# A fixed instruction order from the output projection to the first FFN products

## The chip, the cores and the metric

The kernel runs on one core of one Trainium2 chip. Five engines work beside each other, each taking its own instructions in order: TensorE (PE in the profile, PEld for its weight loads), VectorE (DVE), ScalarE (ACT), GpSimd (POOL) and SyncE (SP, which here issues DMAs). The metric is the device time of one execution in microseconds (us), a median over several; less is better.

## The reference

One layer of a transformer-like block on a sequence of 1024 tokens with 1024 channels, all in float32. What matters here is the passage from the mixer's end to the FFN's entry:

```
x = x + g1 * (merged @ w_out)                       # output projection, gated residual
h = rmsnorm(x, ln2_g) * (1.0 + sc2) + sh2           # modulated norm
f = (silu(h @ w_ffn_gate) * (h @ w_ffn_up)) @ w_ffn_down
x = x + g2 * f
```

`w_out` is 1024 x 1024, `w_ffn_gate` and `w_ffn_up` are 1024 x 2816. Before this stand the mixer's input projection, attention and a gated convolution, which the change does not touch.

## The kernel before

Activations are held transposed: 128 channels on the partitions, tokens along the free axis, in two halves of 512 tokens (n = 0, 1). Channel tiles are counted by m or k from 0 to 7.

Every float32 matrix product is made of three passes with operands rounded to the tensor engine's fp32r format: each operand is split into a high part (ScalarE copies it into an fp32r tile, `whi` for a weight) and a low part (VectorE subtracts the high part from the source, `wlo`), and hi x hi, hi x lo and lo x hi are added in one PSUM bank. A product of the output projection is `mm_ch`: 8 channel tiles x 3 matmuls of 128 x 512. PSUM has eight banks, all handed out under the name `e` by `bank()`.

The output projection is made tile by tile (`wo_tile(m, n)`): all eight m for token half 0, then all eight for half 1, with the split weights `wo` kept for the second half. After each product VectorE forms the new residual `x1` (tiles `xb`, line 1055), ScalarE squares it (line 1062), POOL adds the squares into `acc` (line 134, the line of the helper `tt`), and `x1` is written to DRAM. With m = 7 the squares are summed over the channels by small matmuls with a column of ones (lines 1068, 1069), turned into 1/rms by VectorE and by a power on POOL (lines 120, 121, `rs_m`, `rs_r`), and spread over the partitions by matmuls with the identity (line 1073). `norm2` (line 1078) multiplies `x1` by it, and `split_b` (lines 1082, 1083) adds the shift and splits.

The FFN's two input matrices are multiplied by a Strassen-Winograd scheme: tokens, channels and hidden columns are halved, and seven half products (`half_prod`: 4 channel tiles x 3 matmuls, lines 129 to 131) give the four blocks of a pair of hidden column tiles (j, j + 11). Each half product takes one of seven activation factors, in tiles `rh[q]`, `rl[q]` (high and low parts; some of them in tiles named `big`), and one of seven weight factors. Activation factors 0 and 1 are the two channel halves of token half 0; 2 is a block of token half 1; 3 to 6 are sums of blocks, formed in place in `xb` by VectorE and POOL (lines 1139 to 1157). Weight factors s1 to s4 are sums of blocks that POOL forms in tiles `ws` (line 134). `strassen(j, e, src)` does one column pair for the gate (e = 0) or up (e = 1) matrix; before the factors of token half 1 exist, three pairs of products (`PRE`: (0,0), (0,1), (1,0)) with factors 0 and 1 are made ahead. Memory is reused stage by stage: the tiles `ws` lie where `xb` was.

The order of instructions on each engine is found by a planner that simulates the program as it is traced and takes the earliest traced instruction that it holds to be ready. `in_order(i0)` is a helper that already serves the kernel's first stage: it ties every instruction traced since `i0` to the one before it on the same engine, so that these keep the order in which they are written. The three lines that carry the small sums in the code before:

```python
        ss = bank()
        ...
        r = rstd_of(ss[:, :4], 1.0 / D, dp, 4, eng=nc.vector)
        rb = bank()
```

They stand at the end of `wo_tile` and so directly behind the product of m = 7.

Of the kernel before, what the change touches and what calls it, by code (L numbers as in the profile page):

```python
# [28 lines left out]
def block_kernel(tc, x, x_t, cols, ada_1, ada_2, ada_row, w_q, w_kv, w_v1, w_cg, w_a, w_b, w_o, w_g, w_u, w_d, out):  # L29
# [85 lines left out]
    def rstd_of(ss, scale, pool, w, r=None, eng=nc.gpsimd):  # L115

        m = pool.tile([P, 8], F32, tag="rs_m", bufs=3, name=nm("rs_m"))
        if r is None:
# [2 lines left out]
        nc.gpsimd.tensor_tensor(out=r, in0=m[:, :w], in1=nhalf[:, :w], op=ALU.pow)
        return r
# [723 lines left out]
    def mm_ch(ps, w, ah, al, k0=0, k1=KT):  # L846

        for k in range(k0, k1):
            wh, wl = (v[:, (k % 4) * P:(k % 4 + 1) * P] for v in w[k // 4])
# [1 line left out]
            nc.tensor.matmul(ps, wh, rh_, start=(k == 0), stop=False)  # L851
            nc.tensor.matmul(ps, wh, rl_, start=False, stop=False)  # L852
            nc.tensor.matmul(ps, wl, rh_, start=False, stop=(k == KT - 1))  # L853
# [172 lines left out]
    def split(src):  # L1026

        hi = wp.tile([P, 512], F32R, tag="whi", bufs=9, name=nm("whi"))
        lo = wp.tile([P, 512], F32R, tag="wlo", bufs=9, name=nm("wlo"))
        nc.scalar.activation(hi, src, AF.Copy)  # L1030
        nc.vector.tensor_tensor(out=lo, in0=src, in1=hi.bitcast(F32), op=ALU.subtract)  # L1031
# [2 lines left out]
    def tail_raw(m):
        raw = wp.tile([P, 1024], F32, tag="raw", bufs=3, name=nm("raw"))
        nc.sync.dma_start(raw, w_o[m])
        return raw
# [9 lines left out]
    def wo_tile(m, n):  # L1047

        xi = dp.tile([P, 512], F32, tag="xr", bufs=2, name=nm("xr"))
        ns = slice(n * 512, n * 512 + 512)  # L1050
# [11 lines left out]
        nc.scalar.activation(sq, x1, AF.Square)  # L1062
# [4 lines left out]
        for i in range(4):
            nc.tensor.matmul(ss[:, i:i + 1], acc[n][:, i * P:(i + 1) * P], onec, start=True, stop=False)
            nc.tensor.matmul(ss[:, i:i + 1], sq[:, i * P:(i + 1) * P], onec, start=False, stop=True)
        r = rstd_of(ss[:, :4], 1.0 / D, dp, 4, eng=nc.vector)  # L1070
        rb = bank()
        for i in range(4):
            nc.tensor.matmul(rb[:, i * P:(i + 1) * P], r[:, i:i + 1].broadcast_to([P, P]), ident, start=True, stop=True)
        return rb
# [8 lines left out]
        nc.vector.scalar_tensor_tensor(out=lo, in0=x1, scalar=mod[:, 2, m:m + 1], in1=hi.bitcast(F32), op0=ALU.add,  # L1083
                                       op1=ALU.subtract)

    for m in range(KT):
        if m:
            if m < 7:
                raw = tail_raw(m)
                wo += [split(raw[:, c * 512:(c + 1) * 512]) for c in range(2)] if m < 5 else []  # L1090
                if m >= 5:
                    split_wo(raw, dp, 6)
            else:
                split_wo(tail_raw(m), dp, 6)
        rb = wo_tile(m, 0)
# [3 lines left out]
    NJ = NH // 2  # L1099

    def prod(ps, w, q):
        half_prod(ps, w, rh[q], rl[q])

    def load_pair(j, src):
        return load_raw(src[j]), load_raw(src[j + NJ])
# [10 lines left out]
    for g, (j, e) in enumerate(PRE):
        raw = load_raw((w_g, w_u)[e][j])
        p1, p2 = bank(), bank()
        prod(p1, split(raw[:, :512]), 0)
        prod(p2, split(raw[:, 512:]), 1)  # L1120
        if g < 2:
            c11, c21 = ctile(f"c0{e}", cpa), ctile(f"c1{e}", cpa)
            nc.scalar.activation(c21, p1, AF.Copy)
            tt(nc.vector, c11, p2, c21, ALU.add)
            pre[j, e] = (c11, c21)
        else:
            pre[j, e] = (p1, p2)
# [14 lines left out]
    for j in range(4):
        split_b(rh[2][:, j], rl[2][:, j], 4 + j, norm2(4 + j, 1, rb1))
    stt = nc.vector.scalar_tensor_tensor
    xs = lambda e, n, j: xb[e][n][:, j]
    for j in range(4):
        b01 = norm2(j, 1, rb1)
        stt(out=xs(1, 1, j), in0=xs(1, 1, j), scalar=dsh2[:, j:j + 1], in1=b01, op0=ALU.add, op1=ALU.subtract)
        tt(nc.gpsimd, b01, b01, xs(0, 0, j), ALU.subtract)
        stt(out=xs(0, 0, j), in0=xs(0, 0, j), scalar=mod[:, 2, j:j + 1], in1=xs(1, 1, j), op0=ALU.add, op1=ALU.add)  # L1150
        split_f(5, j, xs(0, 0, j))
# [13 lines left out]
    def strassen(j, e, src):  # L1165

        raw = load_raw(src[j])
        a11, a12 = raw[:, :512], raw[:, 512:]
# [19 lines left out]
        c12, c22 = ct(f"c2{e}", 1), ct(f"c3{e}", 1)  # L1188
        p6 = bank()
        prod(p6, split(s2), 5)  # L1190
        tt(nc.vector, c21, p6, c21, ALU.add)
        p5 = bank()
        prod(p5, split(s1), 4)
        tt(nc.vector, c12, p5, c21, ALU.add)
        p7 = bank()
        prod(p7, split(s3), 6)
        tt(nc.vector, c22, p7, c12, ALU.add)
        tt(nc.vector, c21, p7, c21, ALU.add)
        p3 = bank()
        prod(p3, split(s4), 2)  # L1200
        tt(nc.vector, c12, p3, c12, ALU.add)
        p4 = bank()
        prod(p4, split(a22), 3)
        tt(nc.vector, c21, p4, c21, ALU.add)
# [225 lines left out]
```

## Time and profile before

| | |
|---|---|
| time, median of 3 runs | 1906.98 us (1903.57 to 1910.53) |
| profiled execution: time, span | 1906.22 us, 1904.4 us |
| mean granted TensorE clock | 0.984 |
| TensorE busy | 1821.6 us, 96% of the span |
| VectorE, ScalarE, POOL busy | 1333.8, 776.9, 412.6 us |

The span runs from the first instruction's start to the last one's end. The stretch that the change touches lies between about 1138 us (first product of the output projection) and 1320 us (second column pair of the FFN). A row of a timeline gives start, duration, engine, line, operation and what it writes and reads; behind it, in brackets, how long the engine had stood idle and what ended that. A matmul's shown duration overlaps the next one's, so the step from start to start is its real cost. A row of windows gives the stretch, its length, busy time and count for each of PE, PEld, DVE, ACT and POOL, the granted clock, the share of DMA time and GB/s.

### The profile page before, as it was taken

Reading aid. Unit: us, or ns where it says so; the run is one execution under the profiler, and the core shown is the slowest. Engines: PE = TensorE matmul, PEld = TensorE weight load, DVE = VectorE, ACT = ScalarE, POOL = GpSimd, SP = SyncE. Lnnn points to the kernel's source line nnn. Section 1 sums busy time; section 2 is a strip of 40 time slices with the busy share of each in tenths; the row PEclk is TensorE's granted clock in tenths of the full one; section 3 lists DMA queues with packets and bytes.
Section 4 is the critical chain, followed back from the end, with each engine's and each line's share of the span. In section 5 each row is a group of like instructions: output and inputs, shape, how many; then the busy total and the mean of one; then the engine's idle time right before and its main releaser. Section 6 shows DMA issues by size and latency. Waiting matters only on the chain.

```text
span 1904.4 us, 24641 instructions
## 1 busy us (share of the span) xinstructions
PE 1821.6 (96%) x8781; PEld 1510.2 (79%) x8781; DVE 1333.8 (70%) x1895; ACT 776.9 (41%) x1458; POOL 412.6 (22%) x291
## 2 busy tenths in 40 slices
PE   7999999999999999989999999959999999999999
PEld 5787778887788988777888887748888888878787
DVE  6863867779845888877887543479888778743953
ACT  4342643333434655554655322234344434422221
POOL 1043338232320000000000001145544454300000
PEclk9999999999999999999999999979999999999999
DMA  9598542239549556667453545304344334389676
GB/s 388 205 305 285 170 162 83 77 112 326 188 139 241 145 167 176 179 221 238 128 155 106 195 138 166 111 33 149 142 168 162 143 135 169 128 334 322 240 232 221
DMA packets 153968, 351.42 MB, mean 185 GB/s; under 512 B 15195, under 2 KB 54381, under 8 KB 151670
## 3 DMA queue, kind: packets, MB, share of 16 engines
q1 hardware_dynamic: 93888, 234.82, 38.6%
q10 hardware_dynamic: 58950, 111.36, 16.2%
q0 software_dynamic: 1008, 3.67, 0.5%
q8 instruction: 70, 1.15, 0.3%
q14 instruction: 52, 0.43, 0.1%
HBM read 240.21 MB, written 109.58 MB: 184 GB/s over the span
## 4 chain that ended last, share of the span: by engine, by line
PE 78%; DVE 9%; DMA 6%; issue 3%; ACT 1%; POOL 1%; SPq 0%; ACTq 0%; DVEq 0%; POOLq 0%
PE e L129 7%; PE e L130 7%; PE e L131 7%; PE pj L129 5%; PE pj L130 5%; PE pj L131 5%; PE pj L292 5%; PE pj L851 4%; PE pj L852 4%; PE pj L853 4%; PE e L1273 3%; PE e L1271 3%; PE e L1272 3%; PE tr L784 3%; PE o L800 2%
## 5 line engine op out<-in xcount | busy, mean ns | idle before, releaser
L769 DVE TENSOR_TENSOR_SCAN pt<-pt,mk 128x128 f32<-128x128 f32 (+7 forms) x128 | 172.2, 1351 | 55.1 <-ACT pt L765 54.5
L134 POOL TENSOR_TENSOR acc<-acc,sq 128x512 f32<-128x512 f32 x12 | 15.5, 1291 | 660.6 <-ACT sq L1062 660.6
L129 PE MATMUL e<-big,whi 128*128 128x512 f32 x352 | 138.7, 394 | 18.9 <-ACT whi L1030 18.9
L765 ACT ACTIVATE pt<-z,rq 128x512 f32<-128x512 f32 (+1 forms) x192 | 107.9, 579 | 103.8 <-PE z L764 48.7
L134 DVE TENSOR_TENSOR c<-e,c 128x512 f32<-128x512 f32 x154 | 103.2, 683 | 56.2 <-PE e L131 56.0
L130 PE MATMUL e<-big,whi 128*128 128x512 f32 x352 | 138.4, 393 | 0.0
L131 PE MATMUL e<-big,wlo 128*128 128x512 f32 x352 | 138.1, 392 | 0.0
L129 PE MATMUL pj<-big,whi 128*128 128x512 f32 x320 | 125.1, 391 | 4.4 <-ACT whi L468 2.6
L130 PE MATMUL pj<-big,whi 128*128 128x512 f32 x320 | 124.7, 390 | 0.0
L131 PE MATMUL pj<-big,wlo 128*128 128x512 f32 x320 | 124.3, 390 | 0.0
L1271 PE MATMUL e<-f,whi 128*128 128x512 f32 (+1 forms) x319 | 122.6, 385 | 1.7 <-ACT whi L1030 1.3
L1272 PE MATMUL e<-f,whi 128*128 128x512 f32 (+1 forms) x319 | 122.6, 384 | 0.0
L134 POOL TENSOR_TENSOR ws<-raw,raw 128x512 f32<-128x512 f32 x42 | 61.1, 1456 | 279.3 <-DMA raw<-w_cg 132.2
L1273 PE MATMUL e<-f,wlo 128*128 128x512 f32 (+1 forms) x319 | 116.9, 385 | 3.4 <-DVE wlo L1031 3.4
L134 DVE TENSOR_TENSOR wlo<-raw,whi 128x512 fp32r<-128x512 f32 x124 | 92.9, 756 | 37.3 <-ACT whi L468 29.8
L134 DVE TENSOR_TENSOR c<-pj,c 128x512 f32<-128x512 f32 x140 | 92.9, 682 | 32.8 <-PE pj L131 32.6
L292 PE MATMUL pj<-whi,big 128*128 128x512 f32 x352 | 110.6, 400 | 2.9 <-ACT big L275 2.9
L468 ACT ACTIVATE whi<-raw 128x512 fp32r<-128x512 f32 x116 | 72.4, 628 | 93.3 <-PE pj L130 47.7
L788 DVE TENSOR_TENSOR atl<-tr,ath 128x512 fp32r<-128x512 f32 (+1 forms) x192 | 99.6, 548 | 12.5 <-ACT ath L787 10.9
L787 ACT ACTIVATE ath<-tr 128x512 fp32r<-128x512 f32 (+1 forms) x192 | 87.0, 489 | 49.2 <-PE o L799 30.1
L784 PE MATMUL tr<-dm,pt 128*128 128x128 f32 x576 | 96.3, 276 | 10.3 <-DVE atl L788 10.1
L851 PE MATMUL pj<-big,whi 128*128 128x512 f32 x256 | 105.5, 412 | 0.0
(241 smaller groups left out, 5008.1 us busy)
## 6 DMA issues: line engine op xcount, KB each, us to landing
f<-d_f SPq DMA_DIRECT2D x77, 512.0 KB, 4.3
d_f<-fs ACTq DMA_DIRECT2D x70, 512.0 KB, 2.6
raw<-w_cg SPq DMA_DIRECT2D x40, 512.0 KB, 3.6
raw<-w_g SPq DMA_DIRECT2D x24, 512.0 KB, 3.3
raw<-w_u SPq DMA_DIRECT2D x23, 512.0 KB, 3.3
ad<-ada ACTq DMA_DIRECT2D x19, 512.0 KB, 4.9
ada<-ada SPq DMA_DIRECT2D x8, 1024.0 KB, 10.3
d_t<-ts SPq DMA_DIRECT2D x16, 512.0 KB, 5.3
```

Source lines behind the costliest of these rows:

```text
L129: nc.tensor.matmul(ps, wh[:, k, :], fh[:, k, :], start=(k == 0), stop=False)
L130: nc.tensor.matmul(ps, wh[:, k, :], fl[:, k, :], start=False, stop=False)
L131: nc.tensor.matmul(ps, wl[:, k, :], fh[:, k, :], start=False, stop=(k == 3))
L134: eng.tensor_tensor(out=out, in0=a, in1=b, op=op)
L292: nc.tensor.matmul(ps, a, b, start=(k == 0 and q == 0), stop=(k == KT - 1 and q == 2))
L765: nc.scalar.activation(pt[:, off + s0:off + s0 + m], z[:, :m], AF.Sigmoid, scale=rq[:, 1, i, h:h + 1])
L769: nc.vector.tensor_tensor_scan(out=pt[:, rev], data0=pt[:, rev], data1=mk[:, rev], initial=1.0, op0=ALU.mult, op1=ALU.max)
L784: nc.tensor.transpose(tr[:, j * P:(j + 1) * P], pt[:, off + (b0 + j) * P:off + (b0 + j + 1) * P], ident)
L851: nc.tensor.matmul(ps, wh, rh_, start=(k == 0), stop=False)
L1271: nc.tensor.matmul(o, wh, f[:, 0, c], start=(j == 0), stop=False)
L1272: nc.tensor.matmul(o, wh, f[:, 1, c], start=False, stop=False)
L1273: nc.tensor.matmul(o, wl, f[:, 0, c], start=False, stop=(j == NJ - 1))
```

## The change

The whole passage, from the first output projection product to the last half product of the first column pair, is written out in the order in which each engine is to take it, and tied by `in_order`.

- Token half 0: weight tile m + 3 is loaded and weight tile m + 2 split ahead of product m. The residual's input `xr` is loaded from SyncE's queue instead of ScalarE's, one product ahead.
- Small sums: `sum2` stands behind the product after the last one of its token half, and `spread2` one product behind that. For half 0 the last square is added into `acc` by POOL, so that `sum2` has one partner instead of two.
- Token half 1: the FFN weights of four pairs (`PRE` gains (1,1)) are loaded, and split from product 2 to 5; the normalisation and split of half 0 run from product 2 on; the weight sums s1 to s4 of the first column pair are formed in the raw tiles themselves (and one tile `s2`) instead of in `ws`.
- Factors: in place of one factor after another over all four channel tiles, the work goes by column tile j, in small functions (`n_b22`, `n_b12`, `l_b22`, `f_t3`, `f_t2`, `f_lo`), between the half products. The combination for factor 3 is done by POOL with a shift that ScalarE has added earlier.
- The order of half products of pair (0,0) is p3, p6, p5, p7, p4 and no longer p6, p5, p7, p3, p4, behind eight products made ahead instead of six. Its five combinations follow in `strassen`.

```diff
+    def split_next():
+        hi, lo, src = pend_split.pop(0)
+        nc.scalar.activation(hi, src, AF.Copy)
+        tt(nc.vector, lo, src, hi.bitcast(F32), ALU.subtract)
+    def plan_split(src, pool=None, bufs=9):
...
+        pend_split.append((hi, lo, src))
+        return hi, lo
...
-        nc.scalar.dma_start(xi, x_t[m, :, ns])
+        nc.sync.dma_start(xi, x_t[m, :, n * 512:n * 512 + 512])
...
+    def sum2(n, parts):
+        ss = bank()
...
+    def spread2(r):
+        rb = bank()
...
+    xis = {(0, 0): load_xi(0, 0)}
+    wo_weights(1)
+    wo_weights(2)
+    split_next()
+    split_next()
     for m in range(KT):
...
+        nxt = (m + 1, 0) if m + 1 < KT else (0, 1)
+        xis[nxt] = load_xi(*nxt)
+        if m + 3 < KT:
+            wo_weights(m + 3)
+        for _ in range(2 if m + 2 < KT else 0):
+            split_next()
+        ps = wo_prod(m, 0)
+        wo_end(m, 0, ps, xis.pop((m, 0)))
...
+    PRE = [(0, 0), (0, 1), (1, 0), (1, 1)]
...
+    todo = {2: (0,), 3: (1, 2), 4: (3,), 5: (4, 5), 6: (6,), 7: (7,)}
     for m in range(KT):
-        rb1 = wo_tile(m, 1)
-        split_b(bh[:, m], bl[:, m], m, norm2(m, 0, rb))
+        if m + 1 < KT:
+            xis[m + 1, 1] = load_xi(m + 1, 1)
+        if m < 3:
+            pre_weights(m)
+        elif m == 3:
+            pre_weights(3)
+        elif m == 4:
+            ra = load_raw(w_g[0])
+        elif m == 5:
+            rc = load_raw(w_g[NJ])
+        for k in todo.get(m, ()):
+            split_b(bh[:, k], bl[:, k], k, norm2(k, 0, rb))
+            if k >= 4:
+                nc.scalar.activation(xs(1, 0, k - 4), xs(1, 0, k - 4), AF.Identity, bias=mod[:, 2, k:k + 1])
+        if 2 <= m < 6:
+            split_next()
+            split_next()
+        if m == 6:
+            a11, a12, a21, a22 = ra[:, :512], ra[:, 512:], rc[:, :512], rc[:, 512:]
+            s1, s2, s3, s4 = a21, wp.tile([P, 512], F32, name="s2"), a11, a12
+            tt(nc.gpsimd, s3, a11, a21, ALU.subtract)
+            tt(nc.gpsimd, s2, a22, s3, ALU.subtract)
+        ps = wo_prod(m, 1)
+        if m == 0:
+            r = sum2(0, (acc[0],))
+        elif m == 1:
+            rb = spread2(r)
+        sq = wo_end(m, 1, ps, xis.pop((m, 1)))
+    tt(nc.gpsimd, s4, a12, s2, ALU.subtract)
+    tt(nc.gpsimd, s1, a21, a22, ALU.add)
...
+    p1 = pre_prod(0, 0)
+    r = sum2(1, (acc[1], sq))
+    p2 = pre_prod(0, 1)
+    nc.scalar.activation(ca[0][1], p1, AF.Copy)
+    tt(nc.vector, ca[0][0], p2, ca[0][1], ALU.add)
+    rb1 = spread2(r)
...
+    p1 = pre_prod(1, 0)
...
+    def f_t3(j):
+        stt(out=xs(1, 1, j), in0=xs(1, 1, j), scalar=dsh2[:, j:j + 1], in1=xs(0, 1, j), op0=ALU.add, op1=ALU.subtract)
+        tt(nc.gpsimd, xs(0, 1, j), xs(0, 1, j), xs(0, 0, j), ALU.subtract)
+    def f_t2(j):
+        stt(out=xs(0, 0, j), in0=xs(0, 0, j), scalar=mod[:, 2, j:j + 1], in1=xs(1, 1, j), op0=ALU.add, op1=ALU.add)
+        nc.scalar.activation(rh[5][:, j], xs(0, 0, j), AF.Copy)
...
+    wq6 = plan_split(s2)
+    split_next()
+    p2 = pre_prod(1, 1)
+    nc.scalar.activation(ca[1][1], p1, AF.Copy)
+    tt(nc.vector, ca[1][0], p2, ca[1][1], ALU.add)
+    pre[0, 1] = ca[1]
+    n_b12(1)
+    f_t2(0)
+    l_b22(1)
+    f_t3(1)
+    n_b22(2)
+    f_lo(5, 0, xs(0, 0, 0))
+    pre[1, 0] = pre_prod(2, 0), pre_prod(2, 1)
...
+    p3 = bank()
+    prod(p3, wq4, 2)
     for j in range(4):
...
+        nc.scalar.activation(rh[4][:, j], xs(0, 1, j), AF.Copy)
+        if j == 0:
+            f_lo(5, 3, xs(0, 0, 3))
+        f_lo(4, j, xs(0, 1, j))
+        tt(nc.gpsimd, xs(1, 0, j), xs(1, 0, j), xs(0, 0, j), ALU.subtract)
+    c11, c21 = ca[0]
+    p6 = bank()
+    prod(p6, wq6, 5)
+    wq5 = plan_split(s1)
+    split_next()
     for j in range(4):
         split_f(6, j, xs(1, 1, j))
+    tt(nc.vector, c21, p6, c21, ALU.add)
+    p5 = bank()
+    prod(p5, wq5, 4)
+    wq7 = plan_split(s3)
+    split_next()
     for j in range(4):
-        stt(out=xs(1, 0, j), in0=xs(1, 0, j), scalar=mod[:, 2, 4 + j:5 + j], in1=xs(0, 0, j), op0=ALU.add, op1=ALU.subtract)
         split_f(3, j, xs(1, 0, j))
+    p7 = bank()
+    prod(p7, wq7, 6)
+    wq4 = plan_split(a22)
+    split_next()
+    p4 = bank()
+    prod(p4, wq4, 3)
+    in_order(i0)
```

More of the change, by code (lines that the diff above doesn't have):

```diff
@@ L1032, in split @@
         return hi, lo
[L1034 to L1037, printed above, removed]
+    pend_split = []
+    def split_next():
[3 more added lines that the diff above has]
+    def plan_split(src, pool=None, bufs=9):
+        pool = pool or wp
+        hi = pool.tile([P, 512], F32R, tag="whi", bufs=bufs, name=nm("whi"))
+        lo = pool.tile([P, 512], F32R, tag="wlo", bufs=bufs, name=nm("wlo"))
+        pend_split.append((hi, lo, src))
+        return hi, lo
     a2 = const.tile([P, 8], F32, name="a2")
@@ L1045, in block_kernel, with load_xi, wo_prod, wo_end @@
     acc = [None, None]
-    def wo_tile(m, n):
+    def load_xi(m, n):
         xi = dp.tile([P, 512], F32, tag="xr", bufs=2, name=nm("xr"))
-        ns = slice(n * 512, n * 512 + 512)
-        nc.scalar.dma_start(xi, x_t[m, :, ns])
+        nc.sync.dma_start(xi, x_t[m, :, n * 512:n * 512 + 512])
+        return xi
+    def wo_prod(m, n):
         ps = bank()
         mm_ch(ps, wo[2 * m:2 * m + 2], mh[n], mlo[n])
+        return ps
+    def wo_end(m, n, ps, xi):
         x1 = xb[m // 4][n][:, m % 4, :]
         nc.vector.scalar_tensor_tensor(out=x1, in0=ps, scalar=gmod[:, 0, m:m + 1], in1=xi, op0=ALU.mult, op1=ALU.add)
-        nc.scalar.dma_start(d_x1[m, :, ns], x1)
         if m == 0:
             acc[n] = dp.tile([P, 512], F32, tag="acc", bufs=2, name=nm("acc"))
-            nc.scalar.activation(acc[n], x1, AF.Square)
-            return
-        sq = dp.tile([P, 512], F32, tag="sq", bufs=2, name=nm("sq"))
+            sq = acc[n]
+        else:
+            sq = dp.tile([P, 512], F32, tag="sq", bufs=2, name=nm("sq"))
         nc.scalar.activation(sq, x1, AF.Square)
-        if m < KT - 1:
+        nc.scalar.dma_start(d_x1[m, :, n * 512:n * 512 + 512], x1)
+        if 0 < m < KT - n:
             tt(nc.gpsimd, acc[n], acc[n], sq, ALU.add)
-            return
+        return sq
+    def sum2(n, parts):
         ss = bank()
         for i in range(4):
-            nc.tensor.matmul(ss[:, i:i + 1], acc[n][:, i * P:(i + 1) * P], onec, start=True, stop=False)
-            nc.tensor.matmul(ss[:, i:i + 1], sq[:, i * P:(i + 1) * P], onec, start=False, stop=True)
-        r = rstd_of(ss[:, :4], 1.0 / D, dp, 4, eng=nc.vector)
+            for q, s in enumerate(parts):
+                nc.tensor.matmul(ss[:, i:i + 1], s[:, i * P:(i + 1) * P], onec, start=(q == 0), stop=(q == len(parts) - 1))
+        return rstd_of(ss[:, :4], 1.0 / D, dp, 4, eng=nc.vector)
+    def spread2(r):
         rb = bank()
@@ L1084, in split_b, with prod, wo_weights @@
                                        op1=ALU.subtract)
-    for m in range(KT):
[L1087 to L1095, printed above, removed]
+    NJ = NH // 2
+    def prod(ps, w, q):
+        half_prod(ps, w, rh[q], rl[q])
+    i0 = len(nc.cur_bb.bb.instructions)
+    stt = nc.vector.scalar_tensor_tensor
+    xs = lambda e, n, j: xb[e][n][:, j]
+    def wo_weights(m):
+        raw = load_raw(w_o[m])
+        for c in range(2):
+            k = 2 * m - 2 + c
+            wo.append(plan_split(raw[:, c * 512:(c + 1) * 512], *(() if k < 9 else (dp, 5))))
+    xis = {(0, 0): load_xi(0, 0)}
[3 more added lines that the diff above has]
+    split_next()
+    for m in range(KT):
+        nxt = (m + 1, 0) if m + 1 < KT else (0, 1)
[6 more added lines that the diff above has]
+        wo_end(m, 0, ps, xis.pop((m, 0)))
     bh, bl = big(), big()
@@ L1098, in block_kernel, with pre_weights @@
     rl = [bl[:, 0:4], bl[:, 4:8], None, None, None, None, None]
[L1099 to L1105, printed above, removed]
-    for m in range(KT):
-        rb1 = wo_tile(m, 1)
-        split_b(bh[:, m], bl[:, m], m, norm2(m, 0, rb))
-    PRE = [(0, 0), (0, 1), (1, 0)]
-    held, pre = {}, {}
+    PRE = [(0, 0), (0, 1), (1, 0), (1, 1)]
+    pw = []
+    def pre_weights(g):
+        j, e = PRE[g]
+        raw = load_raw((w_g, w_u)[e][j])
+        pw.append((plan_split(raw[:, :512]), plan_split(raw[:, 512:])))
@@ L1113, in ctile, with split_f @@
+    tt(nc.gpsimd, s4, a12, s2, ALU.subtract)
+    tt(nc.gpsimd, s1, a21, a22, ALU.add)
+    def split_f(q, j, x1, eng=None):
+        nc.scalar.activation(rh[q][:, j], x1, AF.Copy)
+        tt(eng or nc.vector, rl[q][:, j], x1, rh[q][:, j].bitcast(F32), ALU.subtract)
     def ctile(tag, pool=None):
         return (pool or cp).tile([P, 512], F32, tag=tag, bufs=1, name=nm(tag))
[L1116 to L1127, printed above, removed]
+    pre = {}
@@ L1129, in block_kernel, with pre_prod @@
+    def pre_prod(g, half):
+        ps = bank()
+        prod(ps, pw[g][half], half)
+        return ps
+    ca = [(ctile(f"c0{e}", cpa), ctile(f"c1{e}", cpa)) for e in range(2)]
+    wq4 = plan_split(s4)
+    split_next()
[5 more added lines that the diff above has]
+    rb1 = spread2(r)
     s6.close()
@@ L1136, in block_kernel @@
         rl[q] = ep.tile([P, 4, 512], F32R, name=f"rl{q}")
-    def split_f(q, j, x1):
-        nc.scalar.activation(rh[q][:, j], x1, AF.Copy)
-        tt(nc.vector, rl[q][:, j], x1, rh[q][:, j].bitcast(F32), ALU.subtract)
-    for j in range(4):
[L1143 to L1151, printed above, removed]
@@ L1152, in block_kernel, with n_b22, n_b12, l_b22 @@
-    for j in range(4):
-        split_f(4, j, xs(0, 1, j))
+    p1 = pre_prod(1, 0)
+    def n_b22(j):
+        norm2(4 + j, 1, rb1)
+        nc.scalar.activation(rh[2][:, j], xs(1, 1, j), AF.Identity, bias=mod[:, 2, 4 + j:5 + j])
+    def n_b12(j):
+        norm2(j, 1, rb1)
+    def l_b22(j):
+        stt(out=rl[2][:, j], in0=xs(1, 1, j), scalar=mod[:, 2, 4 + j:5 + j], in1=rh[2][:, j].bitcast(F32), op0=ALU.add,
+            op1=ALU.subtract)
+    def f_t3(j):
+        stt(out=xs(1, 1, j), in0=xs(1, 1, j), scalar=dsh2[:, j:j + 1], in1=xs(0, 1, j), op0=ALU.add, op1=ALU.subtract)
+        tt(nc.gpsimd, xs(0, 1, j), xs(0, 1, j), xs(0, 0, j), ALU.subtract)
@@ new lines, in f_t2, with f_lo @@
+    def f_t2(j):
+        stt(out=xs(0, 0, j), in0=xs(0, 0, j), scalar=mod[:, 2, j:j + 1], in1=xs(1, 1, j), op0=ALU.add, op1=ALU.add)
+        nc.scalar.activation(rh[5][:, j], xs(0, 0, j), AF.Copy)
+    def f_lo(q, j, src, eng=nc.vector):
+        tt(eng, rl[q][:, j], src, rh[q][:, j].bitcast(F32), ALU.subtract)
+    n_b22(0)
+    n_b12(0)
+    n_b22(1)
+    l_b22(0)
+    f_t3(0)
+    wq6 = plan_split(s2)
+    split_next()
+    p2 = pre_prod(1, 1)
+    nc.scalar.activation(ca[1][1], p1, AF.Copy)
@@ new lines, in block_kernel @@
+    tt(nc.vector, ca[1][0], p2, ca[1][1], ALU.add)
[7 more added lines that the diff above has]
+    pre[1, 0] = pre_prod(2, 0), pre_prod(2, 1)
+    n_b12(2)
+    f_t2(1)
+    l_b22(2)
+    f_t3(2)
+    n_b22(3)
+    f_lo(5, 1, xs(0, 0, 1))
+    n_b12(3)
+    pre[1, 1] = pre_prod(3, 0), pre_prod(3, 1)
+    f_t2(2)
+    l_b22(3)
+    f_t3(3)
+    f_lo(5, 2, xs(0, 0, 2))
+    f_t2(3)
+    p3 = bank()
+    prod(p3, wq4, 2)
@@ L1165, in strassen @@
     def strassen(j, e, src):
+        c12, c22 = ct(f"c2{e}", 1), ct(f"c3{e}", 1)
+        if (j, e) == (0, 0):
+            c11, c21 = ca[0]
+            tt(nc.vector, c12, p5, c21, ALU.add)
+            tt(nc.vector, c22, p7, c12, ALU.add)
+            tt(nc.vector, c21, p7, c21, ALU.add)
+            tt(nc.vector, c12, p3, c12, ALU.add)
+            tt(nc.vector, c21, p4, c21, ALU.add)
+            return c11, c12, c21, c22
         raw = load_raw(src[j])
         a11, a12 = raw[:, :512], raw[:, 512:]
-        if (j, e) in pre and j == 0:
+        if (j, e) == (0, 1):
             c11, c21 = pre[j, e]
@@ L1187, in strassen @@
         tt(nc.gpsimd, s4, a12, s2, ALU.subtract)
[L1188 to L1204, printed above, removed]
+        q6 = bank()
+        prod(q6, split(s2), 5)
+        tt(nc.vector, c21, q6, c21, ALU.add)
+        q5 = bank()
+        prod(q5, split(s1), 4)
+        tt(nc.vector, c12, q5, c21, ALU.add)
+        q7 = bank()
+        prod(q7, split(s3), 6)
+        tt(nc.vector, c22, q7, c12, ALU.add)
+        tt(nc.vector, c21, q7, c21, ALU.add)
+        q3 = bank()
+        prod(q3, split(s4), 2)
+        tt(nc.vector, c12, q3, c12, ALU.add)
+        q4 = bank()
+        prod(q4, split(a22), 3)
+        tt(nc.vector, c21, q4, c21, ALU.add)
         return c11, c12, c21, c22
```

1 line of the change is left out of this document (added).

## The prediction

> **What bounds the kernel now.** I read the page first, then the waits in the stretch that the diff touches (output projection to the first FFN products), its timeline at each wait, and a table of windows. Among all engines' waits from 1136 to 1300 us (total, times, longest) these two matter:
>
> ```profile
> span 1904.4 us, 24641 instructions
> PE 1821.6 (96%) x8781; PEld 1510.2 (79%) x8781; DVE 1333.8 (70%) x1895; ACT 776.9 (41%) x1458; POOL 412.6 (22%) x291
> ```
>
> ```profile
> PE e L129 <- ACT whi L1030: 18.9, 1, 18.9
> ...
> POOL ws L134 <- DVE big L134: 13.7, 1, 13.7
> ```
>
> ```profile
> 1138.20:1182.50 44.30, 43.31 (x191) 35.42 (x190) 16.30 (x25) 13.43 (x23) 7.75 (x6) 1.00 0.57 191
> 1182.50:1189.50 7.00, 3.88 (x26) 3.71 (x25) 0.91 (x2) 0.63 (x1) 1.02 (x1) 0.85 0.22 76
> 1184.04:1187.45 3.41, 1.72 (x14) 1.64 (x14) 0.16 (x1) 0.43 (x1) 0.92 (x1) 1.00 0.45 156
> 1187.45:1190.87 3.42, 3.27 (x12) 2.98 (x13) 1.16 (x2) 0.37 (x1) 0.09 (x1) 0.50 0.00 0
> 1257.50:1276.80 19.30, 0.41 (x2) 0.00 (x0) 15.57 (x26) 6.61 (x12) 6.38 (x4) 0.63 0.07 27
> 1276.80:1283.00 6.20, 6.20 (x15) 4.85 (x16) 3.60 (x5) 2.03 (x4) 2.59 (x3) 0.50 0.48 157
> 1283.00:1320.00 37.00, 37.00 (x165) 30.62 (x164) 31.81 (x38) 16.17 (x29) 25.65 (x18) 1.00 0.34 120
> ```
>
> TensorE's longest wait, 18.9 us, is for a split weight whose source (`ws`) POOL could form only when the factors in `big` were done (13.7). TensorE bounds the whole kernel (96% busy), so what can be won is its idle time, and in this stretch it has some. The windows' columns are length, then busy time and count of PE, PEld, DVE, ACT, POOL, then clock. Dense work costs 43.31/191 = 0.227 us a matmul: 5.44 us for an output-projection product (24 matmuls), 2.72 us for an FFN half product (12). While TensorE stands still from 1257.5 to 1276.8, VectorE is busy 15.57 of 19.30 us: it makes the factors that the next product needs.
>
> ```profile
> 1143.34 0.39 PE L852 MATMUL e<-big,whi 128*128 128x512 f32 x1
> 1144.71 0.50 PE L853 MATMUL e<-big,wlo 128*128 128x512 f32 x1 [0.99 <-DVE wlo L1031]
> 1145.05 0.39 PE L851 MATMUL e<-big,whi 128*128 128x512 f32 x1
> ...
> 1182.48 0.28 PE L1068 MATMUL e<-onec,acc 128*128 128x1 f32 x2
> 1184.53 0.38 PE L1069 MATMUL e<-onec,sq 128*128 128x1 f32 x2 [1.77 <-ACT sq L1062]
> ...
> 1185.89 0.36 PE L1069 MATMUL e<-onec,sq 128*128 128x1 f32 x2
> 1187.60 2.08 PE L1073 MATMUL e<-dm,rs_r 128*128 128x128 f32 x8 [1.35 <-POOL rs_r L121]
> 1189.33 0.77 PE L851 MATMUL e<-big,whi 128*128 128x512 f32 x1
> ...
> 1233.79 0.28 PE L1068 MATMUL e<-onec,acc 128*128 128x1 f32 x2
> ...
> 1240.63 0.77 PE L129 MATMUL e<-big,whi 128*128 128x512 f32 x1
> 1242.06 0.40 PE L129 MATMUL e<-big,whi 128*128 128x512 f32 x1
> ...
> 1257.53 0.39 PE L131 MATMUL e<-big,wlo 128*128 128x512 f32 x1
> 1276.80 0.79 PE L129 MATMUL e<-big,whi 128*128 128x512 f32 x1 [18.89 <-ACT whi L1030]
> ```
>
> Time in which no product advances, read from start to start: (a) 1143.34 to 1145.05, 1.71 us for two steps of 0.23: 1.3 lost. (b) The sum over channels and the spread of its result after the first token half: 1182.48 to 1189.33 is 6.85, and the clock then stays at half until 1190.87, 0.8 more: 7.6. (c) The same after the second half: 1233.79 to 1240.63 is 6.84, and 1240.63 to 1242.06 holds three steps (0.68) in 1.43: 7.6. (d) 1257.76 (1257.53 and one step) to 1276.80 is 19.0, and then 6.2 us at clock 0.50, half of it lost: 22.1. Together **38.6 us**.
>
> **The change, part by part.**
> *First token half in a fixed order.* Weights are split two products ahead, before the `x1` instruction of the running product on VectorE. (a) came from the reverse order (the split stood behind an `x1` that waited for TensorE). It goes: gain 1.3. What moves: the `xr` loads go from ACT's queue to SP's, ahead of the next weight load, so SP waits for `xr`'s buffer until product m-1 is evicted. The weight behind it is wanted three products (16 us) later and takes:
>
> ```profile
> raw<-w_o SPq DMA_DIRECT2D x8, 512.0 KB, 4.5
> raw<-w_u SPq DMA_DIRECT2D x23, 512.0 KB, 3.3
> ```
>
> Hidden: cost 0; if a landing took over 13.5 us it would show (a rival below).
>
> *Small sums one product later.* In (b) the sixteen one-column passes took 1.8 us (0.11 each: twelve from 1184.53 to 1185.89), the eight passes of the spread 1.73 at half clock. The Square, accumulate and power that TensorE waited for (1.77 and 1.35) fall beside a 5.44 us product. What stays: with one partner instead of two, eight passes, 0.9, and the spread at full clock 0.9 (between 0.87 and 1.73): 1.8. In (c) sixteen passes and the spread stay, 2.7; the cover is one half product each, 2.72 us, against the 2.05 us from 1182.48 to 1184.53 and the 1.3 us from the last pass to the spread (1184.53 + 1.8 to 1187.60). Gain (b)+(c): 15.2 - 4.5 = 10.7.
>
> *Second half: FFN weights split early.* Per 5.44 us product VectorE gets an `x1`, two weight subtractions and one or two normalise-and-split pairs, up to seven instructions of 0.67 (its price below), 4.7 us, and waits for ACT's high parts of some 0.6 each (13.43/23). The two fullest products come to about 6 us, the others to 3 to 4.5, and eight banks let TensorE run ahead: cost 0. Were that cover gone, the fullest would cost 0.6 each.
>
> *The factors.* From R, when the spread's bank is full, TensorE has eleven half products in the new order before (0,1): (0,1)'s two, (1,0)'s two, (1,1)'s two (new here), p3, p6, p5, p7, p4: 29.9 us. In the old order the sums of weights `ws` lie in memory that `xb` gives up after the last factor; the new one forms them inside the raw tiles earlier, so (d)'s releaser goes. Late next is VectorE. Its instructions from R to the last one that p4 needs: 8 normalisations, 4+4+4 low parts or combinations with a scalar, 16 low parts, 4 weight subtractions, 2 adds: 42.
>
> ```profile
> L1078 DVE SCALAR_TENSOR_TENSOR xb<-xb,a,e 128x512 f32<-128x512 f32 x8 | 5.4, 743 | 3.3 <-PE e L1073 3.3
> L134 DVE TENSOR_TENSOR big<-xb,big 128x512 fp32r<-128x512 f32 x8 | 5.3, 674 | 0.0
> ```
>
> Eight in 5.4 or 5.3 us: 0.67 each, 42 x 0.67 = 28.1 us. Beside them POOL does eight subtractions instead of four, and these hold VectorE up:
>
> ```profile
> 1249.83 6.83 POOL L134 TENSOR_TENSOR xb<-xb,xb 128x512 f32<-128x512 f32 x4 [10.97 <-DVE xb L1148]
> 1250.33 0.68 DVE L134 TENSOR_TENSOR c<-e,c 128x512 f32<-128x512 f32 x1
> 1250.93 2.88 DVE L1148 SCALAR_TENSOR_TENSOR xb<-xb,dsh,xb 128x512 f32<-128x512 f32 x2
> 1253.73 1.78 DVE L134 TENSOR_TENSOR rl<-xb,rh 128x512 fp32r<-128x512 f32 x1
> 1255.43 1.77 DVE L1150 SCALAR_TENSOR_TENSOR xb<-xb,mod,xb 128x512 f32<-128x512 f32 x1
> 1257.13 0.68 DVE L134 TENSOR_TENSOR rl<-xb,rh 128x512 fp32r<-128x512 f32 x1
> ```
>
> From 1250.33 to 1257.13 VectorE got through five instructions, 3.4 us worth, in 6.8: four POOL instructions cost it 3.4, 0.9 each (1.1 where both run back to back, 1.78 - 0.67; 0 for the one that reads PSUM, 0.68). Eight cost 7.2. Moving the four `rh[3]` combinations from VectorE to POOL thus saves 4 x 0.67 and costs 4 x 0.9. [...]
>
> One add waits for TensorE (the (0,1) pair, R+5.4), about 1 us of VectorE idle. So the last low part is there at R + 28.1 + 7.2 + 1 = R+36.3; p4 needs it in its third matmul, and has ten more: R+38.9. Against 29.9 of products that is a stall of 9.0, spread over p6, p5, p7 and p4. Then (0,1): its second raw tile can only load once s3 is split, five instructions before that end (R+32.9); load 3.3, two POOL instructions of 1.29, a high part 0.6 and hand-over: R+39.7, 0.8 later than p4's end. Stall S = **10** in all. Bounds: with no lock at all 28.1 + 1 + 2.6 + 0.8 - 29.9 = 2.6; with 1.1 each and the POOL pair at twice its length 13.4. [...]
>
> *Clock.* In the third and fourth rows of the windows TensorE was busy 1.72 of 3.41 us at full clock, and 3.42 us at 0.50 followed. In the paced stretch it runs at 29.9/39.7 = 75% on average, with single windows lower: 1 us (0 to 5: three windows). [...]
>
> *After the stretch.* VectorE owes the five combinations of (0,0) and all of the SwiGLU work of column 0 while TensorE has 15 half products (40.8 us) where it had 22. From 1283 to 1320 (the windows' last row) VectorE was busy 31.81 us for 38 instructions and 18 of POOL, while TensorE did 13.7 products and never waited. Columns 0 and 1 leave VectorE some 62 instructions and 20 of POOL after p4: 62 x 0.67 + 20 x (31.81 - 38 x 0.67)/18 = 48.6 us, 7.8 too much. Most of it (writing the column's factors out) is not what TensorE waits for. Between 0 and 7.8 I take 2.
>
> Sum: 38.6 - 1.8 - 2.7 - 10 - 1 - 2 = **21 us** gained. The profiled execution took 1906.22 (span 1904.4); the median of the three runs is 0.8 higher. 1906.2 - 21.1 = **1885**.
>
> **The rivals.**
> [...]
> *Half clock and VectorE's lag both paid*: for: (b)'s window. Against: 1283 to 1320 without a wait. 5 + 7.8 in place of 3, S at 11: 1896.
> *The order doesn't hold what it says*: the edges tie only the stretch's own instructions; the planner may slip the work that follows ((0,1)'s splits and sums, column 0's SwiGLU, 27 VectorE instructions) between them. All ahead of p4's low part: 27 x 0.67 = 18 more: 1903, no change. Against: its inputs need p4 or the second raw tile.
> *Slower*: the weight loads in SP's queue behind an `xr` load that waits for an eviction. A landing L over 13.5 us makes each of five products late by L - 13.5; it ends above 1912.7 when five times that exceeds 27, L = 19. For: every load now has a wait ahead of it. Against: 4.5 us median. 1913.
>
> **How the numbers follow.** Main case 0.56, weak lock 0.14, clock and lag 0.18, slipped work 0.07, queue 0.05. Best bounds together (S 2.6, no other cost) give 1874.7, worst (spread at half clock, S 13.4, 5, 7.8) about 1899; 1876 to 1897 leaves out the last two cases and the outer edges. A difference under 0.3% (5.7 us, about what a measurement of this kernel can tell from none) is "same": faster 0.88, same 0.07, slower 0.05.
>
> **What would show it.** Right: no wait at the sums' lines and no 18.9; TensorE continuous to p3; short waits for low parts (`rl`, `wlo` from VectorE) adding to about 9 from p6 to p4, VectorE without idle there, its instructions at 1.7 us beside POOL's. Wrong: one long wait still there, or waits for `raw` or PSUM banks, or waits in columns 0 and 1.

## The result and the profile after

The changed kernel took 1884.26 us (median of four runs, 1881.68 to 1886.79) against 1905.86 for the kernel before (1903.57 to 1910.53) on the same chip: ratio 0.9884, 95% interval 0.9859 to 0.9908. 1885 was predicted, with a range of 1876 to 1897. The profiled execution took 1886.79, its span is below.

The page of the changed kernel, the lines that stood first in the prediction and the two groups in which TensorE now waits (busy, mean ns, idle before and releaser):

```profile
span 1885.0 us, 24619 instructions
PE 1819.2 (97%) x8773; PEld 1507.9 (80%) x8773; DVE 1345.5 (71%) x1891; ACT 777.3 (41%) x1462; POOL 417.2 (22%) x296
...
L129 PE MATMUL e<-big,whi 128*128 128x512 f32 x352 | 138.4, 393 | 6.2 <-ACT whi L1030 2.3
...
L131 PE MATMUL e<-big,wlo 128*128 128x512 f32 x352 | 138.0, 392 | 2.9 <-DVE wlo L134 2.9
```

TensorE's waits from 1130 to 1320 us (total, times, longest): one wait of 18.9 has become six of 0.5 to 2.9, and none is at the small sums (lines 1085 and 1091 now).

```profile
PE e L131 <- DVE wlo L134: 2.9, 1, 2.9
PE e L129 <- ACT whi L1030: 2.3, 1, 2.3
PE e L129 <- ACT big L1227: 2.0, 1, 2.0
PE e L129 <- ACT c L1322: 1.0, 1, 1.0
PE e L129 <- ACT whi L1038: 0.8, 1, 0.8
PE e L130 <- DVE big L134: 0.5, 1, 0.5
```

Windows: the whole output projection (1138.9 to 1228.1), then from shortly before p6 begins to the end of p4:

```profile
1138.90:1228.10 89.20, 89.20 (x401) 73.87 (x400) 43.64 (x57) 30.13 (x50) 20.96 (x16) 1.00 0.49 166
1259.30:1275.20 15.90, 11.35 (x38) 8.42 (x39) 15.61 (x22) 9.33 (x18) 6.38 (x5) 0.79 0.20 61
```

The first has no gap at all: sixteen products of 5.44 us, 1.6 us for the small sum and the spread of the first half (1188.18 to 1188.99, 1194.56 to 1195.37), and half a microsecond of slightly longer steps. In the second VectorE is busy 15.61 of 15.90 us and TensorE 11.35: VectorE sets the pace, as the prediction had it. Its timeline where p6 begins to wait:

```profile
1254.62 0.75 DVE L1222 SCALAR_TENSOR_TENSOR xb<-xb,dsh,xb 128x512 f32<-128x512 f32 x1
1255.29 0.68 DVE L134 TENSOR_TENSOR big<-xb,big 128x512 fp32r<-128x512 f32 x1
1257.15 1.74 DVE L1226 SCALAR_TENSOR_TENSOR xb<-xb,mod,xb 128x512 f32<-128x512 f32 x1 [1.18 <-POOL xb L134]
1259.59 4.97 DVE L134 TENSOR_TENSOR big<-xb,big 128x512 fp32r<-128x512 f32 x4 [0.69 <-ACT big L1227]
```

and POOL's there and ahead of pair (0,1):

```profile
1255.45 7.95 POOL L134 TENSOR_TENSOR xb<-xb,xb 128x512 f32<-128x512 f32 x5 [3.40 <-DVE xb L1222]
1272.92 1.82 POOL L134 TENSOR_TENSOR ws<-raw,raw 128x512 f32<-128x512 f32 x1 [9.52 <-DVE wlo L134]
1274.69 1.29 POOL L134 TENSOR_TENSOR ws<-raw 128x512 f32<-128x512 f32 x1
1275.94 2.63 POOL L134 TENSOR_TENSOR ws<-raw,ws 128x512 f32<-128x512 f32 x2
```

p6's first wait goes back to POOL's subtractions from 1255.45 on: VectorE stood idle 1.18 us for one of them, its next instruction took 1.74 us instead of 0.74 beside another, and ScalarE's high part (`ACT big L1227`) could only follow.

### The profile page after: what moved, and what is told of

Read it like the earlier page. It is cut to its first block, busy times and chain, and to the rows that moved or that the text cites. A ratio compares the mean times of both kernels' runs of the same rounds, so it can differ in the third digit from the quotient of the medians.

```text
span 1885.0 us, 24619 instructions
## 1 busy us (share of the span) xinstructions
PE 1819.2 (97%) x8773; PEld 1507.9 (80%) x8773; DVE 1345.5 (71%) x1891; ACT 777.3 (41%) x1462; POOL 417.2 (22%) x296
## 4 chain that ended last, share of the span: by engine, by line
PE 76%; DVE 10%; DMA 7%; issue 2%; ACT 2%; POOL 1%; SPq 1%; ACTq 0%; DVEq 0%; POOLq 0%
PE e L129 6%; PE e L130 6%; PE e L131 6%; PE pj L129 5%; PE pj L131 5%; PE pj L130 5%; PE pj L292 5%; PE pj L851 4%; PE pj L852 4%; PE pj L853 4%; PE e L1415 3%; PE e L1413 3%; PE e L1414 3%; PE tr L784 3%; PE o L800 2%
## 5 line engine op out<-in xcount | busy, mean ns | idle before, releaser
L134 DVE TENSOR_TENSOR wlo<-raw,whi 128x512 fp32r<-128x512 f32 x144 | 109.9, 773 | 43.3 <-ACT whi L468 28.2
L134 DVE TENSOR_TENSOR c<-e,c 128x512 f32<-128x512 f32 x154 | 103.0, 683 | 49.8 <-PE e L131 48.6
L784 PE MATMUL tr<-dm,pt 128*128 128x128 f32 x576 | 97.3, 278 | 10.5 <-DVE atl L788 10.4
```

Source lines behind the costliest of these rows:

```text
L134: eng.tensor_tensor(out=out, in0=a, in1=b, op=op)
L784: nc.tensor.transpose(tr[:, j * P:(j + 1) * P], pt[:, off + (b0 + j) * P:off + (b0 + j + 1) * P], ident)
```

## The experiments

The lowest and the highest time of one kernel lie 3 to 10 us apart, and part of that lies before the stretch (the first output projection product starts at 1135.9 to 1141.9 us in these traces). So each profile is also read from X, the end of the last output projection product, to the first matmul of pair (0,1), which follows p4 in the changed order. "Length" is from the first output projection product's start to X. The kernel before was timed again beside each group of runs (medians 1905.76 to 1907.47), and each ratio is to the times of its own group.

| kernel | median us | ratio to before (95%) | length | (0,1) begins |
|---|---|---|---|---|
| before | 1905.86 | 1 | 96.3 | |
| changed | 1884.26 | 0.9884 (0.9859 to 0.9908) | 89.2 | X+49.8 |
| sum0_at_once | 1894.81 | 0.9949 (0.9932 to 0.9965) | 95.4 | X+49.8 |
| sum1_at_once | 1890.33 | 0.9920 (0.9904 to 0.9937) | 89.2 | X+55.2 |
| sum1_adds_later | 1887.54 | 0.9899 (0.9884 to 0.9913) | 89.2 | X+50.5 |
| adds_later | 1884.93 | 0.9889 (0.9873 to 0.9906) | 89.2 | X+49.0 |
| sub8_on_vector | 1880.55 | 0.9870 (0.9854 to 0.9887) | 89.2 | X+48.1 |
| pool4_more | 1889.06 | 0.9915 (0.9892 to 0.9937) | 89.2 | X+53.9 |
| three_pairs_ahead | 1893.20 | 0.9923 (0.9902 to 0.9944) | 89.2 | X+49.8 |
| raw4 | 1889.81 | 0.9912 (0.9897 to 0.9926) | 89.2 | X+52.9 |
| all_three | 1887.18 | 0.9897 (0.9883 to 0.9912) | 89.2 | X+51.8 |
| planner_order | 1891.42 | 0.9920 (0.9898 to 0.9941) | 90.5 | |
| old_ws_in_raw | 1896.74 | 0.9944 (0.9925 to 0.9963) | 97.3 | |
| old_sums_later | 1902.18 | 0.9982 (0.9968 to 0.9995) | 91.4 | |

**The small sums.** First half's put back behind its last product:

```diff
+        if m == 0:
+            r = sum2(0, (acc[0],))
+            rb = spread2(r)
         ps = wo_prod(m, 1)
-        if m == 0:
-            r = sum2(0, (acc[0],))
-        elif m == 1:
-            rb = spread2(r)
```

> Changed kernel with the first token half's small sum and spread put back directly behind the last product. Theory (each small sum's cover is worth what it takes away): TensorE waits again for the last square and its addition on POOL (about 2.9 us now, since the last square is added on POOL) and for the power (1.35), and runs some 1.5 us at half clock: 5 to 6 us longer than the changed kernel, near 1890. Rival (VectorE paces the second half anyway and absorbs it): 0 to 2 us.

The waits came back, and the length grew by 6.2 us (95.4 against 89.2); nothing behind X changed. The median is 10.5 us higher, the profiled execution 7.4 (1894.18 against 1886.79); of the latter, 2.9 us lie ahead of the stretch, where the edit changes nothing. Beyond the 6.2 us the difference stays open.

```profile
PE e L1085 <- POOL acc L134: 3.0, 1, 3.0
...
PE e L1091 <- POOL rs_r L121: 1.4, 1, 1.4
```

Second half's put back, with pair (0,0)'s combination moved behind the first factor instructions:

```diff
-    p1 = pre_prod(0, 0)
     r = sum2(1, (acc[1], sq))
-    p2 = pre_prod(0, 1)
...
     rb1 = spread2(r)
+    pa0 = pre_prod(0, 0)
+    p2 = pre_prod(0, 1)
...
     split_next()
+    nc.scalar.activation(ca[0][1], pa0, AF.Copy)
+    tt(nc.vector, ca[0][0], p2, ca[0][1], ALU.add)
```

> Changed kernel with the second token half's small sum and spread directly behind the last product, and pair (0,0)'s combination moved behind the first factor instructions, so that VectorE begins the factors when the spread is done. Theory A (VectorE paces from the spread to p4): the spread is done at about X+6.9 instead of X+8.1 (X: end of the last output projection product), p4 ends about 1 us earlier, so the time is 0 to 1 us less than the changed kernel's although TensorE idles 3.4 us more at the sum; the waits at p6 and p5 shrink by 4 to 5 us. Theory B (the terms add as in the prediction): 4.9 us longer.

(0,1) began 5.4 us later, against theory A. VectorE's timeline shows why: in the fixed order the add of pair (0,1) stands ahead of most of the factors, and it waited for the products that had moved behind the sum.

```profile
1239.52 0.69 DVE L134 TENSOR_TENSOR c<-e,c 128x512 f32<-128x512 f32 x1 [1.67 <-PE e L131]
1244.96 0.69 DVE L134 TENSOR_TENSOR c<-e,c 128x512 f32<-128x512 f32 x1 [4.75 <-PE e L131]
1245.57 0.74 DVE L1096 SCALAR_TENSOR_TENSOR xb<-xb,a,e 128x512 f32<-128x512 f32 x1
```

So the run did not tell the theories apart; the next two try it again. First that add alone moved, then both adds moved and the sum at once:

```diff
-    nc.scalar.activation(ca[1][1], p1, AF.Copy)
-    tt(nc.vector, ca[1][0], p2, ca[1][1], ALU.add)
     pre[0, 1] = ca[1]
...
     f_lo(5, 0, xs(0, 0, 0))
+    nc.scalar.activation(ca[1][1], p1, AF.Copy)
+    tt(nc.vector, ca[1][0], p2, ca[1][1], ALU.add)
```

> Changed kernel with pair (0,1)'s combination (a ScalarE copy and a VectorE add that wait for its second half product) moved seven VectorE instructions later. Theory A (VectorE's line starts at that add, where it stands idle 1.4 us): all later factors, p6, p5 and pair (0,1) come 1.4 to 2 us earlier. Rival (the line is set by POOL's subtractions): 0.

> As the run with the second small sum at once, but with both combinations (pairs (0,0) and (0,1)) moved behind factor instructions, so that VectorE's line no longer waits for the products behind the sum. Theory A (the cover of the second sum is worth nothing in itself; VectorE paces from the spread): pair (0,1) begins at X+47 to X+49 instead of X+55.2, no later than in the changed kernel (X+49.8), though TensorE idles 3.4 us more at the sum. Theory B (the cover is worth its 4.9 us): X+53 to X+55.

Moving the add alone brought (0,1) 0.8 us forward (1.4 to 2 expected), nothing that the time shows. With it moved, the sum at once put (0,1) at X+50.5 instead of X+49.0, neither theory's number (the medians, 2.6 us apart, can't tell this finer). TensorE was done with its first four half products 5.6 us later (X+19.3 against X+13.7): 2.5 us of that are waits at the sum, and most of the rest is the clock, at half from 1230.8 to 1237.7. All but 1.4 us of it was back when (0,1) began. But VectorE was not free to begin in this run either:

```profile
1239.21 0.69 DVE L134 TENSOR_TENSOR wlo<-s,whi 128x512 fp32r<-128x512 f32 x1 [1.26 <-ACT whi L1038]
1241.61 0.69 DVE L134 TENSOR_TENSOR c<-e,c 128x512 f32<-128x512 f32 x1 [1.70 <-PE e L131]
```

Its line began 1.5 us earlier than in adds_later, counted from X, and then stood idle 3.0 us for products behind the sum (the ScalarE copy in the first row had itself waited for TensorE), where adds_later has 0.5 us of idle. That makes up 1.0 of the 1.4 us, so they are not the price of the cover alone: what it is worth when VectorE does not wait for TensorE was not measured.

On the kernel before, the same is seen from the other side, with the small sums alone moved (shortened, the notes added here):

```diff
+        r0 = sum2(0, sq0)      # behind product (0, 1)
+        rb = spread2(r0)       # behind product (1, 1)
+        r1 = sum2(1, sq1)      # behind the first product made ahead
+        rb1 = spread2(r1)      # behind the second
```

> Kernel before with one part of the change alone: the small sum behind the next product and the spread one product later, in both token halves, the planner's order kept. Theory A (the second sum's cover only moves the factors' start, and the wait for the factors grows by as much): only the first half's 5 to 6 us are gained, near 1900. Theory B (the terms add): 10.7 us, near 1895.

4.1 us were gained (0.9982, 0.9968 to 0.9995), nearer to A (5 to 6) than to B (10.7): the length fell by 4.9, and the long wait grew from 18.9 to

```profile
PE e L129 <- ACT whi L1030: 23.6, 1, 23.6
```

**The memory of the weight sums**, the other part alone on the kernel before:

```diff
+        if (j, e) == (0, 0):
+            s1, s2, s3, s4 = a21, wp.tile([P, 512], F32, name="s2"), a11, a12
+        else:
+            s1, s2, s3, s4 = (ct(f"ws{q}", 1) for q in range(4))
...
+        tt(nc.gpsimd, s4, a12, s2, ALU.subtract)
         tt(nc.gpsimd, s1, a21, a22, ALU.add)
-        tt(nc.gpsimd, s4, a12, s2, ALU.subtract)
```

> Kernel before with one part of the change alone: pair (0,0)'s weight sums formed in the raw tiles (and one tile s2) instead of in ws, the planner's order kept. Theory A (the 18.9 us wait is for the memory of ws): p6 begins when its factor is ready, near 1265 us instead of 1276.8; the stretch ends 10 to 13 us earlier, time near 1894. Rival B (it is VectorE's pace): the last factor part is done at 1272.1, so at most 4.7 us.

9.6 us were gained, just under A's lower end and twice what B allowed. What is left of the wait is VectorE's: 3.5 at an add, and low parts of the factors. TensorE's waits there:

```profile
PE e L129 <- DVE c L134: 3.5, 1, 3.5
...
PE e L130 <- DVE big L134: 1.5, 2, 1.3
PE e L130 <- DVE rl L134: 1.5, 2, 0.7
```

**The order itself**: `in_order(i0)` left out.

> Changed kernel without the call of in_order for this stretch: the same instructions, dependencies, tiles and queues, the order left to the planner. Theory A (the order itself carries part of the gain): the wait of the first half's second product for its low part comes back (1.3) and VectorE's factor work is taken in another order, 3 to 8 us longer than the changed kernel. Rival (the restructuring alone, weight sums in the raw tiles and small sums later, carries it): within 2 us of the changed kernel.

The ratio went from 0.9884 to 0.9920. (a)'s wait came back (1.0), the power of the second sum is waited for (1.4), and TensorE waits five times for low parts of factors (7.7):

```profile
PE e L130 <- DVE big L134: 7.7, 5, 2.4
PE e L1091 <- POOL rs_r L121: 1.4, 1, 1.4
PE e L853 <- DVE wlo L134: 1.0, 1, 1.0
```

**Cover**: `PRE` without (1,1).

> Changed kernel with three pairs of products made ahead instead of four ((1,1)'s pair is made later, in its own column). Theory A (VectorE paces p6 to p4, so work in front of it is cover): pair (0,1) begins no earlier than in the changed kernel counted from the end of the output projection, the waits before it grow by about 5 us, and the time by 4 to 6 us. Rival (TensorE's total is what counts): 0 to 1 us.

(0,1) began at X+49.8, exactly as in the changed kernel, with 5.4 us less work in front of it. The time grew by more than expected (ratio 0.9923): the pair's 5.4 us came on later, and the wait at `c` in column 1 was 3.1 instead of 1.0.

**VectorE against POOL.** The eight subtractions moved to VectorE, and four more put on POOL:

```diff
-        tt(nc.gpsimd, xs(0, 1, j), xs(0, 1, j), xs(0, 0, j), ALU.subtract)
+        tt(nc.vector, xs(0, 1, j), xs(0, 1, j), xs(0, 0, j), ALU.subtract)
...
-        tt(nc.gpsimd, xs(1, 0, j), xs(1, 0, j), xs(0, 0, j), ALU.subtract)
...
+    for j in range(4):
+        tt(nc.vector, xs(1, 0, j), xs(1, 0, j), xs(0, 0, j), ALU.subtract)
```

```diff
+    for j in range(4):
+        tt(nc.gpsimd, mk[:, :512], mk[:, :512], mk[:, 512:], ALU.subtract)
```

> Changed kernel with POOL's eight factor subtractions on VectorE. Theory A (a POOL subtraction beside VectorE costs it 0.9 us or more, an own one 0.6 to 0.67): the waits from p6 to p4 shrink by 2 to 3 us; the wait of pair (0,1) for its raw tile may take back half; time 1 to 3 us less. Rival (POOL's help is free): VectorE's line from the spread to p4 grows by 8 x 0.6 = 4.8 us and so does the time.

> Changed kernel with four more POOL subtractions of 128x512 on a constant tile that nothing else uses, behind the eight factor subtractions (output unchanged). Theory A (VectorE and POOL exclude each other): VectorE's low parts there take 1.7 us instead of 0.68, p4 and all behind it come 4 to 4.5 us later; about half may be hidden where VectorE waits. Rival (no exclusion, only longer recorded durations): 0.

Both went the way of A. Eight more instructions on VectorE brought (0,1) forward by 1.7 us; the time is 3.7 us lower, though the two ratios' intervals overlap. Four subtractions that nobody waits for put it back by 4.1 us. TensorE's waits in the second:

```profile
PE e L131 <- DVE wlo L134: 5.9, 1, 5.9
PE e L129 <- ACT whi L1030: 2.7, 1, 2.7
```

**The wait ahead of (0,1)**: four raw tiles, and then this with the two moves above.

```diff
-        raw = wp.tile([P, 1024], F32, tag="raw", bufs=3, name=nm("raw"))
+        raw = wp.tile([P, 1024], F32, tag="raw", bufs=4, name=nm("raw"))
```

> Changed kernel with four raw tiles instead of three (eight split tiles in that pool instead of nine, six instead of five in the other; the split of s4 moved behind the spread). Theory A (the wait ahead of pair (0,1) is for its second raw tile, which loads only once s3 is split): that wait falls from 2.5 us to under 0.7, the time by about 2. Rival (it is VectorE's or POOL's lag): unchanged.

> Changed kernel with POOL's eight factor subtractions on VectorE, the combination of pair (0,1) later, and four raw tiles. If VectorE's line and the raw tile are what is left: pair (0,1) begins at X+44 to X+45.5 instead of X+49.8, time 1878 to 1880, 4 to 6 us under the changed kernel. If something else takes over (the lag of columns 0 and 1): under 3 us.

The wait fell to 0.6 as expected, and yet (0,1) came 3.1 us later, the time 5.5. The next pair's sums, ready early now, ran on POOL beside the low parts that p7 waits for. POOL's and VectorE's timelines with four raw tiles:

```profile
1266.71 1.67 POOL L134 TENSOR_TENSOR ws<-raw,raw 128x512 f32<-128x512 f32 x1 [1.83 <-DVE big L134]
1268.33 1.73 POOL L134 TENSOR_TENSOR ws<-raw 128x512 f32<-128x512 f32 x1
1270.03 3.40 POOL L134 TENSOR_TENSOR ws<-raw,ws 128x512 f32<-128x512 f32 x2
```

```profile
1266.56 0.68 DVE L134 TENSOR_TENSOR wlo<-raw,whi 128x512 fp32r<-128x512 f32 x1
1267.16 6.82 DVE L134 TENSOR_TENSOR rl<-xb,rh 128x512 fp32r<-128x512 f32 x4
1273.90 0.68 DVE L134 TENSOR_TENSOR c<-e,c 128x512 f32<-128x512 f32 x1
```

Four low parts took 6.74 us, start to start, where 2.4 would do: 1.1 us lost for each of POOL's. all_three lost its gain in the same way (one wait of 5.8 us for `wlo` in p7, 3.0 in sub8_on_vector): no better than the changed kernel. sub8_on_vector has the lowest median of all, but how far it beats the changed kernel, these runs do not settle.

## Why the prediction was right

The total was right to 1 us, and the mechanism was right too: from the spread on, VectorE's line and what POOL takes from it pace TensorE, and the memory of `ws` no longer does. Up to X it was right term by term; from X to the first product of the FFN's second matrix the two profiles differ by 13.1 us (449.3 and 436.2) where 14.0 follow from the terms. That the total came so close is in part luck, since single terms were off and made up for each other: the three behind the factors (0.8 + 1 + 2 predicted; 2.5, 0 and 1.2 found), and the three that make up VectorE's line.

- *(a) and (b)*, 1.3 + 5.8 predicted: the length fell by 7.1 us (96.3 to 89.2), and sum0_at_once gives 6.2 for (b) alone.
- *The factors' pace.* 36.3 us from the spread to VectorE's last low part was predicted; the spread's first user starts at 1236.51 and the last `wlo` ends at 1272.38: 35.9. The parts fit less well. VectorE's own work was 27.0 us, not 28.1: from start to start an instruction with a scalar takes 0.66 us and one without 0.60, not 0.67, and there were 43 (the 42 and one more, below). POOL's eight subtractions lengthened VectorE's instructions by 4.8 us, not 7.2. And VectorE was idle for 4.0 us, not 1: 1.18 for POOL and 0.69 for ScalarE (both shown above), some short gaps, and this at the add of (0,1):

```profile
1242.05 0.69 DVE L134 TENSOR_TENSOR c<-e,c 128x512 f32<-128x512 f32 x1 [1.43 <-PE e L131]
```

- *The price of a POOL instruction*, 0.9, is too high for the eight themselves (0.6 each, 0.75 with the 1.18 us wait) and about what the two runs on it give: 1.0 for each of the four more (4.1 us), and 0.8 for each of the eight moved (1.7 us won, and the 0.6 that each costs VectorE). What the prediction calls a lock is this delay: its rows show a low part of 1.78 us beside POOL's subtractions (1253.73) and one of 0.68 behind them (1257.13). No run shows what causes it.
- *The end of p4.* It came 38.9 us after the spread (1275.44, which is 1277.92 less the 2.48 lost there), and 38.9 was predicted. But the last low part at 36.3 and ten matmuls of 0.227 make 38.6, and from the 35.9 found they make 38.1; the other 0.8 us is the clock's. (The upper bound of S, too, is 14.0 by its own terms, not 13.4.)
- *The clock.* It fell from 1.00 to 0.50 at 1262.85 (the two windows below), and 1 us was charged for that, the author's estimate between 0 and 5. Ten matmuls of p5 took 4.2 us instead of 2.3 (1265.82 to 1269.99). p7 and p4 then ran without a wait: p4's last low part was there at 1272.38, and its third matmul, the first to use it, began at 1273.17.

```profile
1271.70 0.68 DVE L134 TENSOR_TENSOR wlo<-raw,whi 128x512 fp32r<-128x512 f32 x1
...
1272.72 0.39 PE L129 MATMUL e<-rh,whi 128*128 128x512 f32 x1
1272.95 0.39 PE L130 MATMUL e<-rl,whi 128*128 128x512 f32 x1
1273.17 0.39 PE L131 MATMUL e<-rh,wlo 128*128 128x512 f32 x1
```

So p4 ended 0.8 us later than VectorE's line asked for. Pair (0,1) lost nothing by it, since it waited for its second raw tile anyway. The window ahead of the fall and the one after, in the changed kernel:

```profile
1259.43:1262.85 3.42, 1.87 (x5) 0.78 (x5) 3.26 (x3) 3.42 (x8) 3.42 (x3) 1.00 0.00 0
1262.85:1266.26 3.41, 0.54 (x2) 0.45 (x2) 3.41 (x5) 3.41 (x8) 0.55 (x1) 0.50 0.00 0
```

TensorE was busy 1.87 of 3.42 us in the first, matmuls counted to their shown ends; ahead of the fall in (b) it was 1.72 of 3.41. But in the window before these two (1256.02 to 1259.44) it was busy only 1.56 of 3.42 us, and the clock in the next was 1.00: how much idle time brings the fall, these traces do not show.
- *The second raw tile* was mis-sized. Its load went out at 1269.44, when predicted (R+32.9), and took 3.4, but POOL took three instructions, not two, to the first sum that is used, the first of them 1.82 us long, 4.3 us instead of 2.6. (POOL's row names VectorE's `wlo` as what it waited for; that had ended at 1272.38, the load landed at 1272.80, and POOL began at 1272.92.) TensorE waited 2.3, not 0.8. The 1.29 us reckoned for one instruction of POOL is 7.75/6, from the prediction's first window; the second of the three took just that.
- *The lag after the stretch*, 2 predicted: one wait of 1.0, for the copy ahead of an add in column 1 (`ACT c`), 1.2 with the slow step behind it.
- *(c) was wrongly separated.* Counted alone, hiding the second sum was priced at 4.9. On the kernel before (old_sums_later) the long wait took it back, growing by 4.7 us. In the changed kernel no run measured it alone. The factors begin with the spread and TensorE waits for them anyway. The total held, since the pace had been counted from the spread.
- *The signs.* There is no wait at the sums' lines, no 18.9, and TensorE ran without one to p6. From p6 to p4 the waits add to 6.2 us, not about 9, and only 3.4 of them are for low parts; the other 2.8 are for high parts from ScalarE, which came late behind VectorE. One wait in column 1, named as a sign of being wrong, did come (1.0).

Of the other cases, the weak lock (S = 2.6: POOL's subtractions delay VectorE hardly at all) did not come true: from the spread to p4's end TensorE took 9.0 us more than its eleven products, and POOL's subtractions took 4.8 us from VectorE directly. Slipped work came to one VectorE instruction (a product of column 0's SwiGLU) in the changed kernel's stretch:

```profile
1244.64 0.68 DVE L134 TENSOR_TENSOR c<-c,c 128x512 f32<-128x512 f32 x1
```

With four raw tiles it did come, but as POOL's work and not VectorE's own.

That (d)'s wait was for the memory of `ws` is shown by old_ws_in_raw (9.6 us). The fixed order adds some 7 us to the restructuring (planner_order, 0.9920 against 0.9884; the intervals overlap a little); its profile shows 4.9 of them, 1.3 in the length and 3.6 from X to the FFN's second matrix (439.8 and 436.2). The load queue of `xr`, the work by column tile and the order of pair (0,0)'s half products were not tried by themselves.
